# A transformer step: the down projection's seven products run from one ordered table, and one PSUM bank in it is added to x by VectorE

## The chip, the cores and the metric

The kernel runs on one core of one Trainium2 chip. Its metric is the device time of one execution in microseconds (us). Five engines matter: TensorE (PE, with its weight loads PEld), VectorE (DVE), ScalarE (ACT), GpSimd (POOL) and SyncE (SP, which here only issues DMAs). Each engine takes its instructions strictly in the order in which the program queues them; engines wait for each other by semaphores.

## The reference, cut to what matters

Two layers of a trunk on 256 context tokens and 1024 latent tokens. The change lies in the last matmul of each layer, the down projection of the feed-forward net:

```python
gate, up = jnp.split(h2 @ w_ffn_in[l], 2, axis=-1)
x = x + g2 * ((jax.nn.silu(gate) * up) @ w_ffn_out[l])     # (tokens, 2816) @ (2816, 1024)
```

## The kernel before

Everything is kept transposed: x is three tiles `xs[0]` (256 context tokens), `xs[1]` and `xs[2]` (512 latent tokens each), each with 8 blocks of 128 rows. The product `silu(gate) * up` was written to DRAM as FS, 22 slices of 128 rows. All matmuls are float32 in three passes: each operand is split into a rounded part hi (ACT, `copy` with a cast) and the rest lo (DVE, `tensor_sub`), and `product` runs lo*hi, hi*lo and hi*hi. A split is thus one ACT cast and then one DVE subtraction.

Per layer the down projection has three parts. `ffn_out(0)` and `ffn_out(2)` multiply slices 0 to 3 the plain way. The **middle part**, which the change rewrites, takes slices 4 to 19 in NC = 4 groups j of four slices. `ffn_out(NF - 2)` does the last two slices and the norm that follows. In the middle part the 1024 latent tokens are seen as two halves and a group's slices as two pairs, and for each pair of output blocks m and m + 4 (m = 0 to 3) seven products stand in for eight. I call one (j, m) a **step**; there are 16 in a layer. A step's TensorE order is the same in both kernels:

- `b21`, `t2`, `t1`: six 128x512 matmuls each; then the context product (24 matmuls of 128x256), then `t3`, `b22`, the next step's `b11`, and `t4`.
- `b11`, `t2`, `t3` and `t4` add up, one after the other, in one PSUM bank `a` (the chain). After each of them the bank's running sum has to be added to x before the next product of the chain may write it: after `b11` to block m of `xs[1]`, after `t2` (the second product) to block m of `xs[2]`, after `t3` (the third) to block m + 4 of `xs[2]`, after `t4` to block m + 4 of `xs[1]`.
- Bank `b` holds `b21`; bank `c` holds `t1`, is read, and then takes `b22` on top and is read again. The context bank is read in two halves.

`onto` (L1506) is such a read on DVE, x += bank * gate, in one instruction. `onto2` (L1510 to L1512) does it in two: ACT scales the bank into a tile `u` (L1511), POOL adds `u` to x (L1512). Before the change the chain's second and third reads use `onto2`.

Each step needs two weight slabs, split hi/lo into `w` tiles (a ring of 4): the plain slab `raw`, and one of four sums of its quarters, which POOL makes **in place** in the same `raw` tile (L190 to L192), so that the sums wait for the plain slab's DVE subtraction and the second split waits for the sums. `raw` has 2 buffers.

Each group needs eight operands of 128x1024 (`slots`, 12 in a ring): `b11`, `b21`, `b22` and the context's `c` are loaded from FS and halved in place by `halve` (ACT L1461, DVE L1462); `t1` to `t4` come from eight POOL subtractions (`op_sum`, L1479) into two `q` tiles and are split by `split` (ACT L109, DVE L110), each in two halves of 512. The POOL subtractions read the loaded `b11`, `b21`, `b22`, so `halve` of these has to wait for them. `out7` writes out by hand at which step the next group's loads, sums and splits stand. Inside the middle part every engine follows the order of the program text (`manual_schedule`); ahead of it and behind it only PE does, and a scheduler places the rest. DMAs of the middle part are issued by SP, in order.

Of the kernel before, what the change touches and what calls it, by code (L numbers as in the profile page):

```python
# [50 lines left out]
def build(tc, d):  # L51
# [60 lines left out]
    queue, ready, steps = [], [], []  # L112
# [62 lines left out]


    def out_sums(src):
        raws = []

        def load():  # L180
            raws.append(raw_slab(src))

        def plain():
            w = wtile()
            split(w[:, 0], w[:, 1], raws[0])
            ready.append(w)

        def quarters():
            r = raws[0].rearrange("p (q c) -> p q c", q=4)
            G.tensor_add(r[:, 3], r[:, 1], r[:, 3])  # L190
            G.tensor_sub(r[:, 0:2], r[:, 3:4].to_broadcast([P, 2, 256]), r[:, 0:2])
            G.tensor_sub(r[:, 1:3], r[:, 1:3], r[:, 0:1].to_broadcast([P, 2, 256]))  # L192

        def sums_():
            w = wtile()
            split(w[:, 0], w[:, 1], raws[0])
            ready.append(w)

        steps.append((load, plain, quarters, sums_))

    def want(l):
# [22 lines left out]
        for f in range(4):  # L224
            add(d["w_fo"][l, f * P:(f + 1) * P])
        for j in range(NC):
            for m in range(4):
                out_sums(d["w_fs"][l, j, m])
        for f in range(4, 6):
            add(d["w_fo"][l, f * P:(f + 1) * P])  # L230
# [343 lines left out]
    for l in range(DEPTH):  # L574
# [890 lines left out]
        def op_load(j):  # L1465
            f = 4 + 4 * j
            for kind, x, c in (("b11", 0, 1), ("b21", 2, 1), ("b22", 2, 2)):
                ld(operand(j, kind)[:, 1], rows_of(f + x, 2, c))
            qs[j] = [qpool.tile([P, 4, 512], F32, tag="q", bufs=2, name=nm("q")) for _ in range(2)]
            for i in range(2):  # L1470
                nc.sync.dma_start(qs[j][i][:, 0], FS[l][f + i, :, CH[2][0]:])


        def op_sum(j, n):
            i, n = divmod(n, 4)
            q = qs[j][i]
# [4 lines left out]
        def op_t(j, kind, part=(0, 1)):  # L1481
            t = ops.get((j, kind))
            if t is None:
                t = operand(j, kind)
            for i in part:
                split(t[:, 0, i], t[:, 1, i], qs[j][i][:, {"t1": 0, "t3": 1, "t2": 2, "t4": 3}[kind]])

        def op_c(j):
            ld(operand(j, "c")[:, 1], rows_of(4 + 4 * j, 4, 0))

        def op_h(j, kind):
            halve(ops[j, kind])
# [26 lines left out]
        def out1(j, m):  # L1519
            w = ready.pop(0)  # L1520
            pa_ = fpsum(512)
            product(pa_, wq(w, 0), opd(j, "b11"))
            onto(1, m, pa_)
            return w, pa_
# [3 lines left out]
        def out7(j, m, w, pa_):  # L1528
            s_ = ready.pop(0)
            last = (j, m) == (NC - 1, 3)  # L1530
            nj = j + 1 if j + 1 < NC else None
            cur = steps.pop(0) if steps and not last else None

            def do(at, *work):
                if nj and m == at:
                    for x in work:
                        x()

            def ctx():
                pc = psum()  # L1540
                for u in range(2):
                    a = wq(w, u) + wq(w, 2 + u)
                    mm3(pc[:, u * 256:(u + 1) * 256],
                        [a[i] + (ops[j, "c"][:, 0, i], ops[j, "c"][:, 1, i]) for i in range(4)])
                for u in range(2):
                    onto(0, m + 4 * u, pc[:, u * 256:(u + 1) * 256])

            pb, pc = fpsum(512), fpsum(512)
# [251 lines left out]
```

## Time and profile before

| | us |
|---|---|
| median of 3 runs (3018.08 to 3023.95) | 3021.41 |
| the profiled execution's own time | 3017.62 |
| its span, first to last instruction | 3015.5 |
| middle part of layer 0, by the PE timeline 1260.42 to 1479.87 | 219.45 |
| middle part of layer 1, 2743.20 to 2964.93 | 221.73 |

The span is cut by the clock of the trace: times below are us from its start. The middle part begins with its first matmul of `b11` and ends with the first matmul of the last `ffn_out`. "[1.42 <-DVE ft L1462]" behind a row means that the engine stood idle for 1.42 us before it and that DVE's instruction of line 1462, which writes `ft`, ended the wait. In the trace `ft` is an operand, `f` a bank, `ps` the context bank, `w` a split slab.

### The profile page before, as it was taken

Reading aid. Unit: us, or ns where it says so; the run is one execution under the profiler, and the core shown is the slowest. Engines: PE = TensorE matmul, PEld = TensorE weight load, DVE = VectorE, ACT = ScalarE, POOL = GpSimd, SP = SyncE. Lnnn points to the kernel's source line nnn. Section 1 sums busy time; section 2 is a strip of 40 time slices with the busy share of each in tenths; the row PEclk is TensorE's granted clock in tenths of the full one; section 3 lists DMA queues with packets and bytes.
Section 4 is the critical chain, followed back from the end, with each engine's and each line's share of the span. In section 5 each row is a group of like instructions: output and inputs, shape, how many; then the busy total and the mean of one; then the engine's idle time right before and its main releaser. Section 6 shows DMA issues by size and latency. Waiting matters only on the chain.

```text
span 3015.5 us, 41230 instructions
## 1 busy us (share of the span) xinstructions
PE 2871.2 (95%) x15608; PEld 2452.5 (81%) x15608; DVE 2007.7 (67%) x3157; ACT 1210.4 (40%) x2047; POOL 998.2 (33%) x980
## 2 busy tenths in 40 slices
PE   7999999999999999998999999999999999999997
PEld 4888898888888888877777888888888888887776
DVE  6777787685666554777868677776856533356777
ACT  4523687264223233233442237762622223332342
POOL 1222200035443332376512222001444433315663
PEclk9999999999999999999999999999999999999999
DMA  6576523543333233422235665444434312251212
GB/s 229 155 225 186 175 72 112 180 137 109 124 110 123 91 102 133 147 76 96 91 105 161 206 170 150 107 135 135 149 107 133 101 62 69 69 211 63 91 67 84
DMA packets 164406, 380.63 MB, mean 126 GB/s; under 512 B 20576, under 2 KB 56688, under 8 KB 163952
## 3 DMA queue, kind: packets, MB, share of 16 engines
q1 hardware_dynamic: 119680, 274.00, 29.1%
q0 software_dynamic: 44240, 103.84, 10.2%
q8 instruction: 122, 2.00, 0.3%
q14 instruction: 76, 0.62, 0.1%
q10 hardware_dynamic: 288, 0.16, 0.0%
HBM read 281.97 MB, written 95.95 MB: 125 GB/s over the span
## 4 chain that ended last, share of the span: by engine, by line
PE 66%; DVE 15%; issue 6%; POOL 5%; DMA 4%; ACT 4%; SPq 0%; DVEq 0%; POOLq 0%; ACTq 0%
PE f L1286 30%; PE f L249 15%; PE pa L249 6%; PE pa L489 4%; PE S L429 3%; PE ps L447 3%; DVE w L110 2%; PE ps L249 2%; POOL q L1479 2%; PE ps L967 1%; DVE stt L433 1%; DVE ft L110 1%; DMA x<-XS 1%; ACT E L436 1%; DVE ft L1462 1%
## 5 line engine op out<-in xcount | busy, mean ns | idle before, releaser
L110 DVE TENSOR_TENSOR w<-raw,w 128x1024 fp32r<-128x1024 f32 x278 | 356.2, 1283 | 284.6 <-ACT w L109 284.0
L1286 PE MATMUL f<-h,w 128*128 128x512 f32 x2112 | 506.3, 390 | 1.1 <-ACT pc L1234 1.1
L109 ACT CAST w<-raw 128x1024 fp32r<-128x1024 f32 x278 | 289.8, 1050 | 489.9 <-POOL raw L192 116.6
L1286 PEld LDWEIGHTS f<-h,w 128*128 128x128 f32 x2112 | 392.4, 188 | 82.1 <-ACT pc L1234 1.9
L1286 PE MATMUL f<-ft,w 128*128 128x512 f32 x1344 | 324.5, 396 | 30.3 <-DVE ft L1462 14.8
L1286 PEld LDWEIGHTS f<-ft,w 128*128 128x128 f32 x1344 | 249.6, 190 | 95.0 <-DVE ft L1462 19.9
L1286 PE MATMUL f<-T,w 128*128 128x512 f32 x1080 | 264.8, 394 | 15.0 <-DVE pc L1389 12.0
L1286 PEld LDWEIGHTS f<-T,w 128*128 128x128 f32 x1080 | 201.7, 188 | 65.1 <-DVE pc L1389 16.1
L1227 POOL DMA_DIRECT2D FS<-sg x132 | 72.8, 552 | 541.7 <-DVE sg L1358 222.2
L249 PE MATMUL pa<-h,w 128*128 128x512 f32 (+1 forms) x1296 | 248.4, 352 | 0.8 <-DVE vn L667 0.8
L249 PEld LDWEIGHTS pa<-h,w 128*128 128x128 f32 x1296 | 211.3, 191 | 32.4 <-DVE vn L667 1.0
L489 PE MATMUL pa<-w,h 128*128 128x512 f32 x912 | 218.6, 397 | 12.5 <-DVE w L110 12.0
L433 DVE TENSOR_REDUCE stt<-S 128x1 f32<-128x1280 f32 x128 | 189.9, 1487 | 57.3 <-PE S L429 57.3
L249 PE MATMUL f<-mix,w 128*128 128x512 f32 (+1 forms) x1152 | 225.0, 355 | 0.0
L489 PEld LDWEIGHTS pa<-w,h 128*128 128x128 f32 x912 | 171.9, 191 | 52.8 <-DVE w L110 10.0
L249 PEld LDWEIGHTS f<-mix,w 128*128 128x128 f32 x1152 | 189.8, 189 | 29.5
L436 ACT ACTIVATE E<-S,stt 128x1280 f32<-128x1280 f32 x128 | 170.5, 1332 | 40.9 <-DVE stt L433 40.9
L447 PE MATMUL ps<-vt,pt 128*128 128x128 f32 x1280 | 178.0, 279 | 5.3 <-ACT pt L973 5.2
L249 PE MATMUL f<-ft,w 128*128 128x512 f32 (+1 forms) x864 | 173.7, 362 | 5.7 <-DVE x L1107 5.7
L249 PEld LDWEIGHTS f<-h,w 128*128 128x128 f32 x1392 | 172.7, 192 | 3.3
L249 PE MATMUL f<-h,w 128*128 128x256 f32 x1392 | 174.1, 283 | 0.0
L429 PE MATMUL S<-kb,aq 128*128 128x512 f32 (+1 forms) x624 | 162.7, 377 | 9.7 <-ACT E L436 4.7
(247 smaller groups left out, 4877.4 us busy)
## 6 DMA issues: line engine op xcount, KB each, us to landing
raw<-w_fi SPq DMA_DIRECT2D x112, 512.0 KB, 3.8
ra<-w_adaT SPq DMA_DIRECT2D x96, 256.0 KB, 2.8
FS<-sg POOLq DMA_DIRECT2D x88, 256.0 KB, 2.3
kb<-KS SPq DMA_DIRECT2D x52, 320.0 KB, 6.6
raw<-w_adaT SPq DMA_DIRECT2D x32, 512.0 KB, 4.0
raw<-w_fs SPq DMA_DIRECT2D x32, 512.0 KB, 3.9
ft<-FS SPq DMA_DIRECT2D x32, 512.0 KB, 6.0
raw<-w_in SPq DMA_DIRECT2D x20, 512.0 KB, 3.6
```

Of the source, the lines that this page charges most:

```text
L109: S.copy(hi, src)
L110: V.tensor_sub(lo, src, hi.bitcast(F32))
L249: PE.matmul(ps, lhsT=a, rhs=b, start=(i == 0), stop=(i == n - 1))
L429: PE.matmul(ps[:, o:o + n], lhsT=aq[:, m, q0:q0 + P], rhs=kb[m][1 - p][:, o:o + n], start=(p == 0), stop=(p == 1))
L433: V.reduce_max(st[:, m:m + 1], ps[:, :nkey], axis=AX.X, negate=True)
L436: S.activation(E, ps[:, :nkey], AF.Exp, bias=st[:, m:m + 1], accum_out=st[:, 2 + m:3 + m])
L447: PE.matmul(o[:, :P], lhsT=pt[:, i * P:(i + 1) * P], rhs=vt(b + i), start=(b + i == 0), stop=(b + i == nk - 1))
L489: PE.matmul(ps, lhsT=a[:, y], rhs=wk[:, z], start=(k == 0 and x == 0), stop=(k == KD - 1 and x == 2))
L967: PE.transpose(T_["tp", b][:, x * P:(x + 1) * P], T_["E"][0][:, (4 * b + x) * P:(4 * b + x + 1) * P], ident)
L1227: nc.gpsimd.dma_start(FS[l][f, :, t0:t0 + n], sg)
L1286: PE.matmul(ps, lhsT=y, rhs=z, start=(first and i == 0), stop=(i == 3 * len(a) - 1), skip_group_check=not first)
L1479: G.tensor_sub(q[:, o], x, y)
```

## The change

`out7`, `out1`, `out_sums` and their helpers go. The order of the middle part now stands in one table, PLAN: four rows for m = 0 to 3, each a list of short names that `steps` walks through; each name is one instruction (or one product). A name's suffix says for which step (`+`, `++`, `+++`: 1 to 3 steps later, `-`: one earlier) or for which group (`.`, `:`, `;`: this one, the next, the one after) the instruction works. With the order these parts change:

- The chain's third read (U3) is one DVE instruction, `onto`, in place of ACT's scaling and POOL's addition. The second (U2 on ACT, A2 on POOL) stays as it was.
- POOL's sums of a slab's quarters go to a tile `s` of their own, in four instructions of 256 columns (before: one of 256, two of 512). The slab is loaded three steps ahead, its sums are made two steps ahead, the sums' split begins two steps ahead.
- The four `t` operands are split by one cast and one subtraction of 1024 columns each (before two of 512), out of one `q` tile for a group (before two, one for each slice).
- Of a group's operands, `b11` and `b21` are loaded two groups ahead, `b22`, `q` and `c` one; their casts and subtractions are spread over the steps one by one.
- The splits of the last `ffn_out`'s slabs and operands stand in the last group.

PE's products and their order stay as they were, but for the last step, whose context product moves to where it stands in all others. Line numbers after the change: DVE reads of banks L1511, slab splits L1497, operand splits L1462 (`t`) and L1469, POOL L1484 to L1490 (quarters), L1452 (operands), L1586 (A2).

```diff
-        def out7(j, m, w, pa_):
...
-            product(pb, wq(w, 2), opd(j, "b21"))
...
-            onto(1, m, pb)
-            do(0, lambda: op_load(nj))
-            product(pa_, wq(s_, 0), opd(j, "t2"), False)
-            if cur:
-                cur[2]()
-            onto2(2, m, pa_)
...
-            product(pa_, wq(s_, 1), opd(j, "t3"), False)
-            onto2(2, m + 4, pa_)
...
-            do(3, lambda: op_h(nj, "b21"), lambda: op_t(nj, "t1"))
...
+        def w_sum(g, n):
+            if not n:
+                sums_[g] = qpool.tile([P, 4, 256], F32, tag="s", name=nm("s"))
+            r, s_ = raws[g].rearrange("p (q c) -> p q c", q=4), sums_[g]
+            if n == 0:
+                G.tensor_add(s_[:, 3], r[:, 1], r[:, 3])
...
+        def w_split(key, src, part):
+            if part == "a":
+                slabs[key] = wtile()
+                S.copy(slabs[key][:, 0], src)
+            else:
+                V.tensor_sub(slabs[key][:, 1], src, slabs[key][:, 0].bitcast(F32))
...
+            elif name[0] == "P":
+                c, u, b = {"1": (1, 0, "a"), "2": (1, 0, "b"), "3": (2, 0, "c"), "4": (1, 4, "a"),
+                           "5": (2, 4, "c")}[name[1]]
+                onto(c, m + u, banks[b, g])
+            elif name in UDVE:
+                onto(2, m + 4, banks["a", g])
+            elif name[0] == "U":
+                banks[name, g] = qpool.tile([P, 512], F32, tag="u", bufs=2, name=nm("u"))
+                S.mul(banks[name, g], banks["a", g], mods[l][:, 5 * KD + m + (4 if name == "U3" else 0), 1:2])
...
+        def steps(j, loads=None):
+            for m, names in enumerate(PLAN):
+                for name in names.split():
...
+UDVE = ("U3",)
...
+    """b21 wa+ P4- q3: sd+ t2a: t2 P2 r0++ t1 U2 wd+ q7: cx P5 ld+++ A2 t2d: r1++ b21d: t3 r2++ r3++ b22 C0
+    U3 C1 b11+ sa++ P3 b22d: t4 cL:""",
```

The names of the table that the text uses: P1, P4 are the chain's first and last reads, P2 bank `b`'s, P5 and P3 bank `c`'s two, C0 and C1 the context bank's; `wa`/`wd` and `sa`/`sd` are cast and subtraction of the plain slab and of the sums; `b21d:` is the subtraction of the next group's operand `b21`; `r0` to `r3` are the quarters' sums, `q0` to `q7` the operands'; `ld` loads a slab, `cL:` an operand.

Two places in the order. First DVE, from the end of group 0's fourth step into group 1's first one. `x_10328`, `x_10332`, `x_10336` are xs[0], xs[1], xs[2]; a number behind `f_` is one bank; `ft_10367`, `ft_10368` and `ft_10370` hold operands, `q_...` the sums behind `t` operands. Before:

```order
L110 TENSOR_TENSOR w_11211<-raw_11054,w_11211 128x1024
L1462 TENSOR_TENSOR ft_10367<-ft_10367 128x1024
L110 TENSOR_TENSOR ft_10368<-q_10864,ft_10368 128x512
L110 TENSOR_TENSOR ft_10368<-q_10865,ft_10368 128x512
L1506 SCALAR_TENSOR_TENSOR x_10336<-f_11151,mod_83,x_10336 128x512
L1506 SCALAR_TENSOR_TENSOR x_10332<-f_11236,mod_83,x_10332 128x512
L1506 SCALAR_TENSOR_TENSOR x_10332<-f_11132,mod_83,x_10332 128x512
L1462 TENSOR_TENSOR ft_10368<-ft_10368 128x1024
L110 TENSOR_TENSOR w_11263<-raw_11158,w_11263 128x1024
L1506 SCALAR_TENSOR_TENSOR x_10332<-f_11253,mod_83,x_10332 128x512
L1506 SCALAR_TENSOR_TENSOR x_10336<-f_11254,mod_83,x_10336 128x512
```

Here `ft_10367` is `b21` of group 1, which PE multiplies first of all in the next step, and three subtractions of operands stand ahead of the first read (P1, `f_11236`) of the next step's chain. After:

```order
L1497 TENSOR_TENSOR w_11141<-s_11072,w_11141 128x1024
L1511 SCALAR_TENSOR_TENSOR x_10336<-f_11172,mod_83,x_10336 128x512
L1462 TENSOR_TENSOR ft_10368<-q_10877,ft_10368 128x1024
L1469 TENSOR_TENSOR ft_10368<-ft_10368 128x1024
L1511 SCALAR_TENSOR_TENSOR x_10336<-f_11134,mod_83,x_10336 128x512
L1511 SCALAR_TENSOR_TENSOR x_10328<-ps_11186,mod_83,x_10328 128x256 x2
L1511 SCALAR_TENSOR_TENSOR x_10336<-f_11172,mod_83,x_10336 128x512
L1511 SCALAR_TENSOR_TENSOR x_10332<-f_11235,mod_83,x_10332 128x512
L1462 TENSOR_TENSOR ft_10368<-q_10877,ft_10368 128x1024
L1511 SCALAR_TENSOR_TENSOR x_10332<-f_11134,mod_83,x_10332 128x512
L1462 TENSOR_TENSOR ft_10368<-q_10877,ft_10368 128x1024
L1511 SCALAR_TENSOR_TENSOR x_10332<-f_11256,mod_83,x_10332 128x512
```

Now `b21` is a step further up, P1 (`f_11235`) stands directly behind the step's other reads, and the operand split after it is `t3`'s; the read of `f_11134` in the fifth row is U3, which DVE did not have before.

Second, POOL over the third step of group 0 (`raw` and `s` are a slab's quarters, `q` operands, `x_10336` the additions to xs[2]). Before:

```order
L190 TENSOR_TENSOR raw_10957<-raw_10957 128x256
L191 TENSOR_TENSOR raw_10957<-raw_10957 128x512
L192 TENSOR_TENSOR raw_10957<-raw_10957 128x512
L1512 TENSOR_TENSOR x_10336<-x_10336,u_11069 128x512
L1479 TENSOR_TENSOR q_10865<-ft_10370,q_10865 128x512
L1512 TENSOR_TENSOR x_10336<-x_10336,u_11118 128x512
L1479 TENSOR_TENSOR q_10865<-q_10865,ft_10367 128x512
L1479 TENSOR_TENSOR q_10865<-ft_10370,q_10865 128x512
```

After:

```order
L1452 TENSOR_TENSOR q_10877<-ft_10367,q_10877 128x512
L1484 TENSOR_TENSOR s_11072<-raw_10986 128x256
L1452 TENSOR_TENSOR q_10877<-ft_10367,q_10877 128x512
L1586 TENSOR_TENSOR x_10336<-x_10336,u_11081 128x512
L1486 TENSOR_TENSOR s_11072<-s_11072,raw_10986 128x256
L1488 TENSOR_TENSOR s_11072<-raw_10986 128x256
L1490 TENSOR_TENSOR s_11072<-raw_10986,s_11072 128x256
```

The addition of the chain's third read is gone, the quarters belong to a later slab, and the operands' sums are done a step sooner.

## Rows read from the trace of the kernel before

**Rows 1.** Windows (us, busy us of each engine, clock, DMA): layer 0's middle part, four steps, layer 1's.

```profile
1260.42:1479.87 219.45, 205.19 (x1058) 171.81 (x1057) 156.09 (x184) 81.26 (x103) 139.28 (x101) 0.99 0.26 85
1376.31:1432.81 56.50, 51.29 (x266) 42.57 (x265) 41.34 (x50) 21.52 (x30) 39.74 (x28) 1.00 0.23 80
2743.20:2964.93 221.73, 205.71 (x1058) 171.81 (x1056) 157.26 (x186) 80.17 (x102) 138.53 (x101) 0.99 0.24 80
```

**Rows 2.** Timeline of PE in a step without a wait (start, us, instructions).

```profile
1337.55 9.71 PE L1286 MATMUL f<-ft,w 128*128 128x512 f32 x42
1347.10 3.04 PE L249 MATMUL ps<-ft,w 128*128 128x256 f32 x24
1349.97 1.32 PE L1286 MATMUL f<-ft,w 128*128 128x512 f32 x5
```

**Rows 3.** Waits of PE in layer 0's middle part (us, times, longest).

```profile
PE f L1286 <- DVE ft L1462: 7.7, 6, 1.5
PE f L1286 <- DVE x L1506: 5.1, 5, 1.1
```

**Rows 4.** Timeline of PE from group 1 to group 2.

```profile
1370.93 1.43 PE L1286 MATMUL f<-ft,w 128*128 128x512 f32 x5 [1.42 <-DVE ft L1462]
1373.45 3.02 PE L1286 MATMUL f<-ft,w 128*128 128x512 f32 x12 [1.10 <-DVE x L1506]
...
1380.83 0.96 PE L1286 MATMUL f<-ft,w 128*128 128x512 f32 x3 [0.55 <-DVE ft L110]
1383.06 8.38 PE L1286 MATMUL f<-ft,w 128*128 128x512 f32 x35 [1.27 <-DVE ft L1462]
```

**Rows 5.** Timeline of DVE in the same stretch.

```profile
1368.58 2.29 DVE L1462 TENSOR_TENSOR ft<-ft 128x1024 fp32r<-128x1024 f32 x1 [1.19 <-POOL q L1479]
1370.80 1.28 DVE L110 TENSOR_TENSOR ft<-q,ft 128x512 fp32r<-128x512 f32 x2
1372.00 2.06 DVE L1506 SCALAR_TENSOR_TENSOR x<-f,mod,x 128x512 f32<-128x512 f32 x3
...
1380.69 2.31 DVE L1462 TENSOR_TENSOR ft<-ft 128x1024 fp32r<-128x1024 f32 x1
```

**Rows 6.** Windows: three us after two waits at the end of group 0.

```profile
1317.00:1320.00 3.00, 3.00 (x8) 2.35 (x8) 3.00 (x4) 0.35 (x1) 0.37 (x1) 0.54 0.33 124
```

**Rows 7.** Timeline of DVE around 1395.

```profile
1395.25 1.22 DVE L110 TENSOR_TENSOR w<-raw,w 128x1024 fp32r<-128x1024 f32 x1
```

**Rows 8.** Timeline of POOL in the same stretch.

```profile
1395.34 2.28 POOL L1479 TENSOR_TENSOR q<-q,ft 128x512 f32<-128x512 f32 x1
1397.58 1.28 POOL L1512 TENSOR_TENSOR x<-x,u 128x512 f32<-128x512 f32 x1
```

**Rows 9.** Line 1506 over the whole trace: shortest/median/longest ns.

```profile
L1506 DVE SCALAR_TENSOR_TENSOR x<-f,mod,x x160: 734/746/754, 1262.6 to 2965.1; 128x512 f32<-128x512 f32 x160
```

**Rows 10.** Groups of DVE in the four steps (busy us, mean ns, idle before).

```profile
L1506 DVE SCALAR_TENSOR_TENSOR x<-f,mod,x 128x512 f32<-128x512 f32 x21 | 15.1, 744 | 4.6 <-PE f L1286 4.6
L110 DVE TENSOR_TENSOR w<-raw,w 128x1024 fp32r<-128x1024 f32 x9 | 12.1, 1347 | 1.5 <-ACT w L109 1.4
L110 DVE TENSOR_TENSOR ft<-q,ft 128x512 fp32r<-128x512 f32 x8 | 7.2, 926 | 1.1 <-ACT ft L109 1.1
L1462 DVE TENSOR_TENSOR ft<-ft 128x1024 fp32r<-128x1024 f32 x4 | 7.0, 1761 | 3.3 <-POOL q L1479 3.3
L1506 DVE SCALAR_TENSOR_TENSOR x<-ps,mod,x 128x256 f32<-128x256 f32 x8 | 3.5, 477 | 4.6 <-PE ps L249 4.6
```

**Rows 11.** Groups of POOL in the four steps.

```profile
L1512 POOL TENSOR_TENSOR x<-x,u 128x512 f32<-128x512 f32 x8 | 11.2, 1401 | 0.5 <-ACT u L1511 0.5
...
L190 POOL TENSOR_TENSOR raw<-raw 128x256 f32<-128x256 f32 x4 | 2.9, 736 | 11.0 <-DVE w L110 11.0
```

**Rows 12.** Waits of all engines in the four steps.

```profile
ACT w L109 <- POOL raw L192: 13.1, 4, 4.6
```

**Rows 13.** DMA issues of layer 0's middle part (median us to landing).

```profile
ft<-FS SPq DMA_DIRECT2D x10, 512.0 KB, 5.3
```

More of the change, by code (lines that the diff above doesn't have):

```diff
@@ L110, in split @@
         V.tensor_sub(lo, src, hi.bitcast(F32))
-    queue, ready, steps = [], [], []
+    queue, ready = [], []
     pools = {}
@@ L173, in sums @@
         queue.extend([gate, up, rest])
[L177 to L199, printed above, removed]
     def want(l):
@@ L1462, in halve, with op_load, q_load @@
             V.tensor_sub(t[:, 1], t[:, 1].bitcast(F32), t[:, 0].bitcast(F32))
[L1465 to L1471, printed above, removed]
+        HALVES = {"b11": (0, 2, 1), "b21": (2, 2, 1), "b22": (2, 2, 2), "c": (0, 4, 0)}
+        SUMS = {"t1": 0, "t3": 1, "t2": 2, "t4": 3}
+        def op_load(j, kind):
+            x, n, c = HALVES[kind]
+            ld(operand(j, kind)[:, 1], rows_of(4 + 4 * j + x, n, c))
+        def q_load(j, i):
+            if not i:
+                qs[j] = qpool.tile([P, 2, 4, 512], F32, tag="q", name=nm("q"))
+            nc.sync.dma_start(qs[j][:, i, 0], FS[l][4 + 4 * j + i, :, CH[2][0]:])
         def op_sum(j, n):
             i, n = divmod(n, 4)
-            q = qs[j][i]
+            q = qs[j][:, i]
             b11, b21, b22 = (ops[j, k][:, 1, i].bitcast(F32) for k in ("b11", "b21", "b22"))
@@ L1479, in op_sum, with op_t @@
             G.tensor_sub(q[:, o], x, y)
-        def op_t(j, kind, part=(0, 1)):
+        def op_t(j, kind, part):
             t = ops.get((j, kind))
@@ L1517, in opd @@
             return [(t[:, 0, i], t[:, 1, i]) for i in range(2)]
[L1519 to L1524, printed above, removed]
-        def out7(j, m, w, pa_):
[L1529 to L1540, printed above, removed]
+        banks = {}
@@ L1656, in build @@
         ffn_out(0, fds[0])
-        op_load(0)
-        op_c(0)
+        steps(-2, True)
+        steps(-1, True)
         ffn_out(2, fds[1])
-        for n in range(8):
-            op_sum(0, n)
-        for kind in ("b11", "b21", "t2", "t1", "c", "t3", "b22", "t4"):
-            (op_t if kind[0] == "t" else op_h)(0, kind)
-        for x in steps.pop(0):
-            x()
-        steps[0][0]()
-        nxt = out1(0, 0)
-        man = ExitStack()
-        man.enter_context(tc.manual_schedule())
-        for j in range(NC):
-            for m in range(4):
-                nxt = out7(j, m, *nxt)
-            if j == NC - 2:
-                for x in range(2):
-                    ld(tf[:, x, 1], FS[l][NF - 2 + x])
-        man.close()
+        steps(-2, False)
+        steps(-1, False)
+        with tc.manual_schedule():
+            for j in range(NC):
+                steps(j)
+            for m, names in enumerate(PLAN):
+                for name in names.split():
+                    if name[-1] == "-" and m < name.count("-"):
+                        step(name.rstrip("-"), 4 * NC + m - name.count("-"))
+        ready.extend(slabs["f", x] for x in range(2))
         fts = [tf[:, x] for x in range(2)]
-        for x in fts:
-            halve(x)
         dq.close()
```

166 lines of the change are left out of this document (117 added, 49 removed).

## The prediction

> **What bounds the kernel now.** I read three things in turn: how long the middle part takes against what its matmuls need, what PE waits for there, and what makes the awaited engine late.
>
> The windows of the two middle parts [rows 1] are 219.45 and 221.73 us long. A step without a wait [rows 2] starts its 42 long matmuls at 1337.55 and its 24 short ones at 1347.10: 9.55 us, 1.364 for a product of six. The 24 short ones take 2.87 more, until the next long one at 1349.97. A step thus needs 9.55 + 2.87 = 12.42 us and 16 steps 198.7. The rest is loss: 219.45 - 198.7 = 20.7 us in layer 0, 221.73 - 198.7 = 23.0 in layer 1, **43.7 us in all, 1.4% of the time**. No order of the other engines can give more in these parts, since PE's work stays.
>
> All that PE waits for there is DVE [rows 3]: 7.7 us on the halving of loaded operands, 5.1 us on the adds to x. These are the idle times alone; PE also loses some time in restarting after each, and after a close pair of waits it ran for 3 us at a granted clock of 0.54 [rows 6], that is mostly at 1.2 in place of 2.4 GHz. All this is inside the 43.7.
>
> Where the waits stand tells their cause. From group 1 to group 2 [rows 4] PE stops four times. At 1370.93 it needs `b21` of the next group, whose subtraction DVE begins only at 1368.58, having waited for POOL, and which takes 2.29 us [rows 5]. Behind it DVE still has two `t1` subtractions (1.28) and then three adds (2.06), of which the chain's first read P1 holds up `t2`: PE stops again at 1373.45. At 1380.83 and 1383.06 it stops for `t3` and `b22` of the group that already runs. So DVE is not short of time, it has its work in the wrong place: in four steps of 56.50 us it is busy for 41.34 [rows 1].
>
> Part of that busy time is waiting too. The halving subtraction of 1024 columns takes 1761 ns on average, 9 slab subtractions 1347 [rows 10], though one alone takes 1.22 us [rows 7]. The POOL instruction that is queued at 1395.34, beside that subtraction, takes 2.28 us where the next one takes 1.28 [rows 8]: the two don't run at once, and the later one stands still until the earlier is through. The adds from PSUM never do this: 160 of them lie between 734 and 754 ns [rows 9]. I call the resource that subtractions and POOL share the gate.
>
> **The change part by part.** Four steps are the unit, a group.
>
> *DVE.* U3 adds 4 instructions to 20 of 0.746 us and 8 of 0.477. With 8 slab and 8 operand subtractions of 1.22 (the four `t` now one of 1024 columns instead of a pair that took 1.28, [rows 5]): 24 x 0.746 + 8 x 0.477 + 16 x 1.22 = 41.2 us. Queued back to back an add takes 0.66 ((2.06 - 0.746)/2, [rows 5]), so 48 instructions overlap by some 0.08 each: 37.4 us net, against 49.7 that PE needs. DVE fits with 12 us to spare, less what it waits at the gate.
>
> *POOL and the gate.* POOL loses 4 adds of 1.28. The quarters become 16 of 0.736 [rows 11] in place of 4 of 0.736 and 8 of 1.28: 11.8 against 13.2 us. Eight operand sums of 1.28 stay. POOL: 11.8 + 5.1 + 10.2 = 27.1 us, before 13.2 + 10.2 + 10.2 = 33.6 (busy 39.74 with its waits, [rows 1]). With DVE's subtractions (19.5; before 8 + 4 of 1.22 and 4 pairs of 1.28, 19.8) the gate is needed for 46.6 us of a group against 53.4 of 56.50 before. It was 95% full and would be 94% full in 49.7 us: this is the tight resource of the new order.
>
> *ACT* gets rid of 4 scalings and is busy for 21.52 of 56.50 [rows 1]; its casts stop waiting for the sums in place (13.1 us a group, [rows 12]), since these are now a step ahead. I cost this at nothing either way: hidden behind PE.
>
> *Loads.* SP gets the same DMAs, other places. The nearest one to its use is the context operand: issued when the third step's last `b11` is through (9.70 + 1.36 = 11.06), landed 5.3 us after issue [rows 13], so at 4.0 of the fourth step; its cast stands behind `t1`'s there (done near 4.6). Hidden, and if it were late by more than about 3 us, DVE would hold U3 up. The two loads that are put two groups ahead reach SP's queue before x is loaded, while SP waits for room for x anyway: nothing.
>
> *Does the new order leave a wait?* Within a step the products begin at 0 (b21), 1.36 (t2), 2.73 (t1), 4.09 (context), 6.97 (t3), 8.33 (b22), 9.70 (next b11), 11.06 (t4). Reads can start some 0.2 us after their product. The operands of the next group are ready long ahead: `b11` after its second step, `b21`, `b22`, `t2` after the third, `t1` and `c` in the fourth, `t3` early in the next group for 6.97, `t4` by about 3.2 for 11.06. That clears the operand waits. What is left is the adds of the chain. In the third step DVE has ahead of U3: P4, P2, P5 (0.66 each), `sd`, `wd`, `t2d`, `b21d` (1.14 each) and C0 (0.40), 6.9 us. Starting at 0.2, with waits of 0.6 to 0.8 at the gate behind three of the four subtractions and one for P5's or a cast's readiness, U3 starts near 9.8 and ends near 10.5, before t4 at 11.06. Starting at 1.0 (the second step ran late at the gate) with three waits of nearly a full POOL instruction (1.0 to 1.2), it ends at 11.5: 0.5 us late. In the fourth step P1, P4, P2, P5, `wd`, `sd`, `t1d`, `cd` come to 7.2 us, the same margin; there P1 stands first for t2 at 1.36 and can be late by 0.3 to 0.8 when `b22d` ended the third step late. The first and second steps hold only 8.7 and 7.7 us of DVE's work (5 and 7 adds, 4 and 2 subtractions, the context's two halves) and let it catch up. So a group loses between 0 and 1.3 us. I take the upper end, since the gate is as full as it was: 1.3 x 3 groups with a successor x 2 layers = 7.8 us; the last group has no next operands, and I take nothing there. At the head, DVE's work ahead of the first step is the same (eight operands, two slabs), so nothing; PE's stops in `ffn_out(2)` stay.
>
> Sum: 43.7 - 7.8 = **35.9 us less**: 3017.6 - 35.9 = 2981.7 by the profiled execution's time. The median of the runs before is 3.8 above that execution, so I expect 2985.5 for a median of runs. Bounds: 43.7 less (2974 and 2977.7) if no wait is left; below.
>
> **The rivals.**
>
> *DVE becomes the bound.* U3 goes from an engine that is busy 21.52 of 56.50 us to one that is busy 41.34. If DVE has no idle time to give, each of the 32 moved adds costs its full 0.66: 21 us back, 14.8 us less than before, 3002.8 (3006.6 for the median). For it: the gate at 94%, DVE's subtractions wait there and its queue is in order. Against it: 12 us net of slack in 49.7. The Trainium skill, "Perfetto Trace Analysis", section "Optimizing Scalar/DVE Operations", says that when DVE is saturated, moving work off it to ScalarE may make sense; the change does the opposite, and by that advice this rival would be the outcome. The busy shares above don't show DVE saturated.
>
> *Slower.* U3 is a new DVE deadline inside every step: t4 may not start before it ends. If U3 came late by L in each of 32 steps, PE loses 32 L. The gain is eaten at L = 43.7/32 = 1.37 us, and at 1.6 the kernel is 7 us slower, 3024 (3028). That needs U3 to end at 12.4 or later of a step of 12.42, two full waits at the gate more than I count, every time; the longest single wait seen is about 1.1 us (2.31 against 1.22, [rows 5]). Unlikely.
>
> *The change doesn't do what it says.* POOL is what made `b21` late (1.19 idle before 1368.58, [rows 5]); if its operand sums still end late, because its queue now holds sums of slabs two steps ahead that wait for a free `s` or a load, the operand subtractions wait as before and only order changes: no difference, 3017 to 3021. Against it: POOL has 6.5 us a group less to do, and the last operand sum now stands early in the third step, a step before its use.
>
> **How the numbers follow.** Forecast 0.75; DVE-bound, with about 15 us less, 0.15; no difference 0.05; slower 0.05. A measurement here can tell about 0.2% (6 us) from no change. Faster: 0.75 + 0.15 = 0.90; within 0.2%: 0.05; slower 0.05. The likeliest case by itself, on the median's scale, lies between 2978 (nothing left of the 43.7) and 2997 (two and a half times the loss I take). The range adds the 3.8 us between execution and median below, and reaches to the DVE-bound case above: 2974 to 3006.
>
> **What would show it.** Right: both middle parts near 203 us long (198.7 + 3.9); PE's waits on operand halving gone, a few on adds to x (U3, P1) of under 1 us in the third and fourth steps; no half-clock stretch; POOL near 27 us busy a group plus its waits; subtractions on DVE still above 1.22 us on average. DVE-bound: PE waits for the adds in most steps, 0.5 to 0.7 each, and DVE near 100% busy there. Wrong altogether: waits of PE on operands, or DVE idle on POOL for over 1 us ahead of U3.

## The result, and the profile after

The changed kernel takes 2980.86 us (median, 2973.67 to 2984.5); in the same session the kernel before took 3022.52 us (3018.08 to 3023.95). The ratio is 0.9862, 95% interval 0.984 to 0.9883: 1.4% faster. The prediction was 2985.5 us in 2974 to 3006, with 0.90 for faster. The profiled execution took 2980.07 us, 37.5 less than that of before; 35.9 was forecast.

The windows of the changed kernel's middle parts, with four steps between them (columns as in [rows 1]):

```profile
1264.20:1464.20 200.00, 199.58 (x1058) 171.91 (x1056) 160.18 (x187) 70.69 (x75) 115.92 (x96) 1.00 0.27 86
1369.26:1418.90 49.64, 49.64 (x264) 42.73 (x263) 42.15 (x49) 16.94 (x18) 33.81 (x29) 1.00 0.19 62
2725.90:2925.84 199.94, 199.52 (x1057) 171.92 (x1056) 160.55 (x188) 69.55 (x74) 116.21 (x96) 1.00 0.25 81
```

The middle parts are 19.45 and 21.79 us shorter than in [rows 1], 41.2 together. The four steps take 49.64 us instead of 56.50, and PE is busy in all of it. The clock is 1.00, so the stretch of [rows 6] is gone. The span is only 37.2 shorter because the rest of the program differs from profile to profile: the first middle part begins at 1264.20 instead of 1260.42. In the changed kernel and e1, e2 and e4 to e7 below, whose programs up to there are all but the same, this beginning lies anywhere between 1258.2 and 1264.2. So the length of the middle parts is the sharper measure, and I compare by it.

The waits of PE in layer 0's middle part of the changed kernel; layer 1's gives the same single row:

```profile
PE f L1255 <- DVE x L1511: 0.4, 1, 0.4
```

[rows 3] has eleven waits there, and leaves out a third row of the same view, two waits on the splits of `t`:

```profile
PE f L1286 <- DVE ft L110: 1.1, 2, 0.5
```

The PE timeline where that wait stands, in the last step:

```profile
1447.61 6.29 PE L1255 MATMUL f<-ft,w 128*128 128x512 f32 x27
1454.32 3.06 PE L1255 MATMUL f<-ft,w 128*128 128x512 f32 x12 [0.42 <-DVE x L1511]
```

And DVE there (timeline): the halving of the last `ffn_out`'s operand (L1431) waits for ACT and then holds up the add behind it.

```profile
1452.11 1.49 DVE L1431 TENSOR_TENSOR ft<-ft 128x1280 fp32r<-128x1280 f32 x1 [1.43 <-ACT ft L1430]
1453.52 2.06 DVE L1511 SCALAR_TENSOR_TENSOR x<-f,mod,x 128x512 f32<-128x512 f32 x3
```

DVE's groups in the four steps, beside those of [rows 10] (busy us, mean ns, idle before):

```profile
L1511 DVE SCALAR_TENSOR_TENSOR x<-f,mod,x 128x512 f32<-128x512 f32 x24 | 17.8, 747 | 4.4 <-PE f L1255 4.1
L1469 DVE TENSOR_TENSOR ft<-ft 128x1024 fp32r<-128x1024 f32 x4 | 6.7, 1665 | 0.0
L1497 DVE TENSOR_TENSOR w<-raw,w 128x1024 fp32r<-128x1024 f32 x5 | 6.5, 1296 | 0.0
L1497 DVE TENSOR_TENSOR w<-s,w 128x1024 fp32r<-128x1024 f32 x4 | 6.1, 1522 | 0.4 <-ACT w L1495 0.4
L1511 DVE SCALAR_TENSOR_TENSOR x<-ps,mod,x 128x256 f32<-128x256 f32 x8 | 3.6, 476 | 2.7 <-PE ps L218 2.7
```

The halvings no longer wait for POOL (0.0, before 3.3). DVE waited for PE before as well (4.6 + 4.6 us in [rows 10], now 4.1 + 2.7); what is gone is its idle time behind ACT and POOL, 5.8 us there and 0.4 here. The subtractions are still longer than the 1.22 us of [rows 7].

### The profile page after: what moved, and what is told of

It is laid out like the page before. It is cut to its first block, busy times and chain, and to the rows that moved or that the text cites. A ratio compares the mean times of both kernels' runs of the same rounds, so it can differ in the third digit from the quotient of the medians.

```text
span 2978.3 us, 41223 instructions
## 1 busy us (share of the span) xinstructions
PE 2865.6 (96%) x15608; PEld 2457.3 (83%) x15608; DVE 2019.1 (68%) x3157; ACT 1187.8 (40%) x1983; POOL 957.2 (32%) x980
## 5 line engine op out<-in xcount | busy, mean ns | idle before, releaser
L110 DVE TENSOR_TENSOR w<-raw,w 128x1024 fp32r<-128x1024 f32 x210 | 265.4, 1266 | 270.1 <-ACT w L109 269.7
L109 ACT CAST w<-raw 128x1024 fp32r<-128x1024 f32 x210 | 218.4, 1050 | 360.1 <-POOL raw L159 107.7
L1255 PE MATMUL f<-ft,w 128*128 128x512 f32 x1344 | 312.7, 390 | 0.8 <-DVE x L1511 0.8
L1511 DVE SCALAR_TENSOR_TENSOR x<-f,mod,x 128x512 f32<-128x512 f32 x192 | 142.0, 747 | 46.4 <-PE f L1255 44.6
```

What stands on the lines that cost most here:

```text
L109: S.copy(hi, src)
L110: V.tensor_sub(lo, src, hi.bitcast(F32))
L1255: PE.matmul(ps, lhsT=y, rhs=z, start=(first and i == 0), stop=(i == 3 * len(a) - 1), skip_group_check=not first)
L1511: V.scalar_tensor_tensor(xs[c][:, m], in0=ps, scalar=mods[l][:, 5 * KD + m, COND[c]:COND[c] + 1], in1=xs[c][:, m], op0=ALU.mult, op1=ALU.add)
```

## The experiments

Each ratio is to the kernel before, timed in the same session. "Lost" is the length of both middle parts less twice 198.7, the need of PE that the prediction worked out (its 43.7 and the 43.8 here differ by rounding). "A part" is one layer's middle part.

| run | median us | ratio to before (interval) | middle parts us | lost us |
|---|---|---|---|---|
| before | 3022.52 | | 219.45, 221.73 | 43.8 |
| changed | 2980.86 | 0.9862 (0.984 to 0.9883) | 200.00, 199.94 | 2.5 |
| e1 | 2983.79 | 0.9867 (0.9853 to 0.9882) | 200.98, 200.99 | 4.6 |
| e2 | 2979.31 | 0.9858 (0.9842 to 0.9874) | 200.82, 200.73 | 4.2 |
| e3 | 3010.72 | 0.9958 (0.9943 to 0.9972) | 212.85, 215.41 | 30.9 |
| e4 | 2975.68 | 0.9839 (0.9825 to 0.9854) | 199.45, 199.48 | 1.5 |
| e5 | 2994.66 | 0.9911 (0.9894 to 0.9927) | 208.29, 208.28 | 19.2 |
| e6 | 2980.25 | 0.9862 (0.9847 to 0.9877) | 200.97, 200.94 | 4.5 |
| e7 | 2986.21 | 0.9877 (0.9862 to 0.9892) | 204.94, 204.98 | 12.5 |
| e8 | 3017.81 | 0.9984 (0.9975 to 0.9994) | 217.86, 219.50 | 40.0 |
| e9 | 2989.79 | 0.9894 (0.988 to 0.9907) | 203.91, 205.49 | 12.0 |
| e10 | 3009.17 | 0.9956 (0.9942 to 0.9969) | 212.71, 215.81 | 31.1 |
| e11 | 2967.05 | 0.9816 (0.9803 to 0.983) | 198.72, 198.72 | 0.0 |
| e12 | 2977.18 | 0.9851 (0.9833 to 0.9868) | 202.57, 202.58 | 7.8 |

**e1: the new table, U3 back on ACT and POOL.** A3 is POOL's add of U3; the same in all four rows.

```diff
-UDVE = ("U3",)
+UDVE = ()
-    ... r2++ U3 r3++ b11+ q0: P3 ...
+    ... r2++ U3 r3++ A3 b11+ q0: P3 ...
```

> The table's order is kept, but the chain's third read goes back to ACT's scaling and POOL's addition (right behind, on POOL). The changed kernel has 41.2 us less in its two middle parts than the one before (200.0 and 199.9 against 219.45 and 221.73). Theory 1 (the order did it: operand subtractions ahead of their products, sums ahead): PE still waits little, middle parts of 200 to 203 us each, 36 to 41 us less than before. Theory 2 (the gate did it: POOL's work that DVE took over is what made room): a group then needs the gate for 46.6 + 4 x 1.28 = 51.7 us, more than the 49.7 of PE, so at least 2.0 us for each of 6 groups come back and most likely more, middle parts of 206 us or longer, at most 29 us less than before.

Windows of layer 0's middle part:

```profile
1262.15:1463.13 200.98, 200.41 (x1057) 171.68 (x1056) 156.29 (x173) 81.38 (x91) 145.58 (x112) 1.00 0.27 86
```

Only 1.0 us a part comes back, with POOL busy for 145.58 us instead of 115.92. So 39.2 of the 41.2 us stay without U3 on DVE, and 2.0 belong to its engine, given this table. The 39.2 belong to the order together with the table's other parts (the slabs' sums earlier and in a tile of their own, `t` split in one piece); e6 and e9 below take some of these apart.

**e2: U2 on DVE as well.**

```diff
-UDVE = ("U3",)
+UDVE = ("U2", "U3")
-    ... U2 wd+ A2 cx P5 ...
+    ... U2 wd+ cx P5 ...
```

> The chain's second read is put on DVE as well; POOL then adds nothing to x. DVE's net work rises from 37.4 to 40.0 us of 49.7 in a group, the gate falls from 46.6 to 41.5. Theory 1 and theory 2: nothing is left to win but about 1.2 us in each middle part, so within 3 us of the changed kernel, 39 to 44 us less than before. Theory 3 (DVE is at its limit): PE waits for adds in the third and fourth steps, 0.5 us or more in each, 8 us or more given back.

Windows of layer 0's middle part:

```profile
1260.74:1461.56 200.82, 199.98 (x1057) 171.86 (x1056) 170.01 (x205) 60.06 (x59) 87.43 (x80) 1.00 0.28 86
```

DVE is now busy for 170.01 of 200.82 us and PE loses 0.8 more a part. DVE is not the bound, even with sixteen more adds a part.

**e3: the kernel before, U3 on DVE.**

```diff
-            onto2(2, m + 4, pa_)
+            onto(2, m + 4, pa_)
```

> The kernel before, its order kept, with the chain's third read as one DVE instruction. Theory 1: the operand subtractions stand where they stood, PE's waits on them stay, at most 10 us less than before, or a few us more since DVE has 2.6 us more to do in a group. Theory 2: the gate is needed for 53.4 - 5.1 = 48.3 us of 49.7, so it fits, and 20 us or more are saved.

The waits of PE in layer 0's middle part:

```profile
PE f L1286 <- DVE ft L1462: 3.8, 3, 1.3
PE f L1286 <- DVE x L1506: 3.2, 4, 1.0
PE f L1286 <- DVE ft L110: 1.6, 3, 0.5
```

It saves 6.6 + 6.3 = 12.9 us, between the two theories. POOL, freed of four adds a group, has b21's sums done sooner (at the turn to group 2 DVE waits 0.53 us for them where it waited 1.19, [rows 5]), and the three waits on `b21` among the six on L1462 in [rows 3] are gone; the three on `b22` are still there. What U3's engine is worth thus depends on the order: 12.9 us in the old one, 2.0 in the table. The two parts of the change don't add up.

**e4: b21's last halving from the third step to the fourth, behind P3.**

```diff
-    ... t2d: r1++ b21d: t3 r2++ ...
+    ... t2d: r1++ t3 r2++ ...
-    ... C1 P3 sa++ t4 P1+ t3d:
+    ... C1 P3 b21d: sa++ t4 P1+ t3d:
```

> The changed kernel with one name moved: the subtraction of the next group's b21 from the third step to the fourth, behind P3, so that it ends near or after the time when PE wants b21. Theory 1: PE waits there for the operand's subtraction once in each of 6 groups, 0.7 to 1.5 us with the restart, 4 to 9 us given back, 33 to 38 us less than before. Theory 2: the gate's load is the same, nothing changes, 40 to 43 us less than before.

Timeline of DVE at the end of a fourth step, and of PE there:

```profile
1357.81 1.22 DVE L1469 TENSOR_TENSOR ft<-ft 128x1024 fp32r<-128x1024 f32 x1
1358.94 0.75 DVE L1511 SCALAR_TENSOR_TENSOR x<-f,mod,x 128x512 f32<-128x512 f32 x1
```

```profile
1354.81 7.43 PE L1255 MATMUL f<-ft,w 128*128 128x512 f32 x32
```

The expected loss did not come: the halving is through at 1359.03 and PE runs on through the turn of the group. It takes its bare 1.22 us there, where in the third step of the changed kernel it took 2.32, and the parts are the shortest so far.

**e5: U3's add behind P3's.** In all four rows of the table.

```diff
-    ... r1++ C1 b22 r2++ U3 r3++ b11+ q0: P3 sa++ t4 ...
+    ... r1++ C1 b22 r2++ r3++ b11+ q0: P3 U3 sa++ t4 ...
```

> The changed kernel with one edit: in all four rows of the table the add of U3 stands behind that of P3 on DVE, instead of ahead of it (b11's sum and P3 in between). In the changed kernel U3's add ends 9.3 to 9.5 us into a step and the product t4, which overwrites its bank, begins at 11.06, so 1.5 us are spare; P3's bank is filled only shortly before. Theory 1 (what the change saves is the order of the work against TensorE's demand, and U3's bank has a deadline with 1.5 us to spare): U3 would end some 0.3 to 0.5 us after t4 wants to begin in each of the 32 steps; with the pipeline's refill 10 to 16 us come back, middle parts of 205 to 208 us, about 2991 to 2997 us. Theory 2 (TensorE's queue absorbs it, U3 has no deadline that matters here): middle parts of 200 to 201 us, the time of the changed kernel within 3 us.

Windows of layer 0's middle part, and one of PE's stops (timeline):

```profile
1258.17:1466.46 208.29, 203.73 (x1057) 170.83 (x1056) 160.55 (x189) 70.72 (x75) 111.26 (x96) 1.00 0.26 83
```

```profile
1348.45 1.88 PE L1255 MATMUL f<-ft,w 128*128 128x512 f32 x7 [0.21 <-DVE x L1511]
```

16.6 us come back, half a microsecond a step on average, a little over the upper end of what theory 1 said. By the starts of the matmuls, 15 steps of this part lose 0.41 to 0.49 us each. The last one, which has no next `b11` between `b22` and t4, loses 1.8. U3's deadline is real, and PE's queue does not absorb it: the slower rival had its mechanism right.

**e6: the slabs prepared one step ahead, as before.** Row 1 of four; the others alike.

```diff
-    """b21 P1 wa+ P4- r0++ t2 P2 r1++ wd+ t1 r2++ U2 r3++ ld+++ cx A2 P5 q1: t3 C0 q5: C1 b22 U3 q2: b11d:
-    b11+ sa++ t4 P3 q6: P1+""",
+    """b21 P1 wa+ P4- r0+ t2 P2 r1+ wd+ t1 r2+ U2 r3+ ld+++ cx A2 P5 sa+ q1: t3 C0 q5: C1 sd+ b22 U3 q2: b11d:
+    b11+ t4 P3 q6: P1+""",
```

> The changed kernel with the slabs' preparation pulled back to one step ahead: the four sums of a slab on POOL and the splits into its high and low parts on ACT and DVE stand all in the step just before the one that uses them, as in the kernel before, instead of being spread over two steps. Everything else, U3 on DVE and the place of the ffn operands, is as in the changed kernel. Theory 1 (the gain is the place of the ffn operands' halvings and sums, which no longer come behind TensorE's demand): the slabs were in time before too, so the middle parts stay at 200 to 204 us and the time within 5 us of the changed kernel. Rival (the deeper pipeline of the slabs is what clears the way): at least 15 us of the 41 come back, 215 to 220 us for both parts' loss together, 2996 us or more.

1.0 us a part comes back, so the deeper pipeline of the slabs is not where the gain lies. The sums keep their own tile here, so this run says nothing of ACT's wait for sums in place ([rows 12]); e9 does.

**e7: b21's last halving behind t3's, at the end of the fourth step.**

```diff
-    ... t2d: r1++ b21d: t3 r2++ ...
+    ... t2d: r1++ t3 r2++ ...
-    ... C1 P3 sa++ t4 P1+ t3d:
+    ... C1 P3 sa++ t4 P1+ t3d: b21d:
```

> The changed kernel with the last halving of b21 (on DVE) at the very end of the fourth step of a group, behind t3's. It ended 0.5 us before TensorE wanted it when it stood behind P3 in that step; at the end of the row it comes some 3 us after that. Theory 1 (a late operand stops TensorE for as long as it is late, and nothing takes that up again): each of the three groups with a successor in a middle part loses about 3 us, 18 to 20 us in both layers, middle parts of 208 to 210 us, about 2998 us: half of the change's gain gone by one misplaced instruction of 1.2 us. Rival (the later steps of the group have the time to catch up, as the prediction said of the first and second steps): the products behind run at once and the middle parts stay at 200 to 203 us.

The waits of PE in layer 0's middle part, and its window:

```profile
PE f L1255 <- DVE ft L1469: 4.6, 3, 1.5
PE f L1255 <- DVE x L1511: 0.4, 1, 0.4
```

```profile
1261.92:1466.86 204.94, 199.94 (x1057) 171.84 (x1056) 156.03 (x189) 70.42 (x75) 111.64 (x96) 1.00 0.27 84
```

One instruction of 1.2 us in the wrong place costs 10.0 us of the 41.2. Theory 1 is right that nothing takes the loss up again; its size was twice too large, since the halving was 1.5 us late and not 3.

**e8: the kernel before, operands sooner.** The sums, splits and halvings of the next group go to earlier steps, but in lumps, where the code had room for them.

```diff
-            do(1, lambda: op_sum(nj, 1))
-            do(2, lambda: op_sum(nj, 4), lambda: op_t(nj, "t2", (0,)))
-            do(3, lambda: op_sum(nj, 7))
-            if j and m == 0:
-                op_t(j, "t3")
-                op_h(j, "b22")
+            do(1, lambda: op_sum(nj, 1), lambda: op_sum(nj, 5))
+            do(2, lambda: op_sum(nj, 3), lambda: op_h(nj, "b11"))
+            do(3, lambda: op_h(nj, "b21"))
...
-            do(2, lambda: op_h(nj, "b11"))
+            do(2, lambda: op_t(nj, "t2"))
```

> The kernel before with its own structure (U3 still through ACT and POOL, slabs prepared one step ahead, plain function calls instead of a table); only the sums, splits and halvings of the next ffn operands are issued at sooner steps of a group: the sums of POOL from the first step on, b11, t2 and b22 in the third step, b21, t1, c and t3 in the fourth, t4 in the next group's first. Theory 1 (order): the waits of TensorE for operand halvings, which make most of the 43.7 us lost in the two middle parts, go, and 20 us or more are saved: middle parts of 208 to 212 us, 2995 to 3003 us. Rival (the work that the change takes from ACT and POOL, and U3's shorter chain, are what counts): at most as much as U3 on DVE alone gave, 13 us: middle parts of 213 to 219 us, 3008 to 3020 us.

The waits of PE in layer 0's middle part:

```profile
PE f L1286 <- DVE x L1506: 6.5, 5, 1.7
PE f L1286 <- DVE ft L110: 5.4, 3, 2.8
PE f L1286 <- ACT ft L109: 1.0, 1, 1.0
```

And one such wait, DVE's timeline and PE's:

```profile
1354.30 2.82 DVE L110 TENSOR_TENSOR ft<-q,ft 128x512 fp32r<-128x512 f32 x2
1357.05 0.74 DVE L1506 SCALAR_TENSOR_TENSOR x<-f,mod,x 128x512 f32<-128x512 f32 x1
```

```profile
1357.84 3.01 PE L1286 MATMUL f<-ft,w 128*128 128x512 f32 x12 [1.73 <-DVE x L1506]
```

Only 3.8 us are saved, and theory 1 as I had put it falls: "sooner" is not enough. The middle parts lie at the upper end of the rival's range (213 to 219); e9 tests its cause. The waits on b21 and b22 (L1462) are gone, and adds to x (6.5 us, before 5.1) and the splits of `t` (L110, 5.4 us, before 1.1) have taken their place: in the rows above, a pair of `t` subtractions stands on DVE ahead of an add that PE wants at once.

**e9: the same sums, the halvings one by one.** They are placed so that none stands directly ahead of an add that PE wants next: t2 behind the third step's last add, b22 early in the fourth step, t1 and c at its end, t3 and t4 early in the next group.

```diff
+            if j and m == 0:
+                op_t(j, "t3")
+            do(3, lambda: op_h(nj, "b22"))
...
+            if j and m == 0:
+                op_t(j, "t4")
...
+            do(2, lambda: op_t(nj, "t2"))
+            do(3, lambda: op_t(nj, "t1"), lambda: op_h(nj, "c"))
```

> The kernel before, with the operand sums as soon as in the run with the operands sooner, but with the halvings set one by one where no add that TensorE needs next stands behind them: b11 and b21 behind the step's first sum-of-slab work, t2 behind the step's last add in the third step, b22 at the start of the fourth, t1 and c at its end, t3 and t4 in the first half of the next group's first step. U3 still goes through ACT and POOL. In the run with the operands sooner the waits had moved from the halvings to the adds that stood behind pairs of halvings on DVE (11 waits on the adds, 14.7 us idle, 6 on halvings, 10.9). Theory 1 (the order decides: sooner, and nothing urgent behind): 25 us or more saved in the two middle parts, 204 to 209 us each, 2985 to 2997 us. Rival (in this structure POOL and the slabs' splits are late whatever the operands' places are, since U3's add sits on POOL): middle parts of 212 to 218 us, 3003 to 3018 us.

The waits of PE in layer 0's middle part:

```profile
PE f L1286 <- DVE x L1506: 3.1, 3, 2.0
```

And one of ACT there:

```profile
ACT w L109 <- POOL raw L192: 48.9, 15, 4.9
```

31.8 of the 43.8 us are saved in the old structure, with U3 on ACT and POOL, slabs one step ahead and sums in place: all waits on operands are gone, three on adds are left. The order alone does it, and this order means both: early enough, and not ahead of an urgent add. The wait of ACT for sums in place is as long as ever (48.9 us, 41.9 in the kernel before), so it was not what cost these 31.8 us.

**e10: e9 with U3 on DVE.** The one line of e3.

> As the run with the halvings one by one, and U3's bank is added to x by DVE. Theory 1 (order alone; U3's engine counts only where the order is bad): within 4 us of the run without it when that one is near 205 us a part. Rival (U3's engine is what clears POOL in this structure): 13 us or more below the run without it, as on the kernel before, middle parts 6 us shorter each.

Both theories missed: it is 19 us slower than e9. Timeline of DVE in a group's first step, and of PE there:

```profile
1378.37 2.82 DVE L110 TENSOR_TENSOR ft<-q,ft 128x512 fp32r<-128x512 f32 x2
1381.12 0.86 DVE L1506 SCALAR_TENSOR_TENSOR x<-ps,mod,x 128x256 f32<-128x256 f32 x2
1381.90 1.21 DVE L110 TENSOR_TENSOR w<-raw,w 128x1024 fp32r<-128x1024 f32 x1
1383.04 2.05 DVE L1506 SCALAR_TENSOR_TENSOR x<-f,mod,x 128x512 f32<-128x512 f32 x3
```

```profile
1377.25 4.27 PE L1286 MATMUL f<-ft,w 128*128 128x512 f32 x18
1383.92 2.88 PE L1286 MATMUL f<-ft,w 128*128 128x512 f32 x7 [2.41 <-DVE x L1506]
```

The 18 matmuls are t3, b22 and the next b11; t3's six are through near 1378.6. U3's add, the first of the three at 1383.04, could start then, but stands behind t4's two splits, the context's adds and a slab's subtraction; t4's product waits for it until 1383.92. In e9 the detour over ACT and POOL went round this queue. The chain's third read on DVE is good only where DVE's row has room in front of it, and the table has that: only one operand's subtraction, `t4`'s, stands ahead of U3 in a group's first step.

**e11: the table with the best places.** e4's move, and the last `ffn_out`'s operands halved behind P5 of the last group's third and fourth steps (ending the wait at 1454.32 above), and the first step's slabs summed and split ahead of `ffn_out(2)` instead of behind it.

```diff
+                                              j == -1 and 4 * j + m + len(sign) == 0 and sign[0] == "+" and
+                                              kind in ("wa", "wd", "sa", "sd", "r0", "r1", "r2", "r3")) != loads:
...
+                    if kind == "P5" and j == NC - 1 and m > 1:
+                        halve(tf[:, m - 2])
```

> The changed kernel with b21's last halving in the fourth step behind P3 (its middle parts were 199.5 us), and two edits around the middle part: the last ffn operands of a layer are halved behind P5 of the last group's third and fourth steps, and in the prologue the first slab's sums and splits go ahead of the splits of the other operands. Theory 1 (the middle part is at its floor of 198.7 plus under 1 us; what is left to save lies at its head and tail): middle parts of 199 to 200 us, the stop of TensorE ahead of the middle part (0.4 and 2.1 us idle, and a stretch at half the clock) shorter by 1 to 3 us a layer, 2970 to 2976 us. Rival (head and tail are set by the loads of x and the last operands, not by this order): 2975 to 2977 us, as without these two edits.

Windows of both middle parts, and of 30 us ahead of the first one, here and in the changed kernel:

```profile
1255.50:1454.22 198.72, 198.72 (x1057) 172.17 (x1056) 157.63 (x188) 70.54 (x75) 116.25 (x96) 1.00 0.27 87
2713.56:2912.28 198.72, 198.72 (x1058) 172.16 (x1056) 157.74 (x187) 69.59 (x74) 116.25 (x96) 1.00 0.25 81
...
1228.00:1258.00 30.00, 30.00 (x156) 25.65 (x156) 28.29 (x35) 8.33 (x10) 16.23 (x11) 1.00 0.12 35
```

```profile
1228.00:1258.00 30.00, 27.49 (x136) 23.12 (x135) 24.35 (x32) 8.42 (x9) 14.97 (x12) 0.94 0.14 52
```

PE never waits in a middle part: 198.72 us each is the floor of 198.7 that the prediction had from one clean step. The stop ahead of it (2.5 us idle) is gone too. The median of 2967.05 us lies below the 2970 to 2976 of theory 1. At 0.9816 this version beats both kernels: the interval ends at 0.983, where the changed kernel's begins at 0.984. Of the 13.8 us to the changed kernel the middle parts explain 2.5, and the stop in `ffn_out(2)` 2.5 idle in layer 0 and 1.8 in layer 1 and its restarts; the rest lies elsewhere in the program and is not settled. In the two profiled executions the first middle part begins at 1255.50 and at 1264.20, so 8.7 us of the difference lie ahead of it.

**e12: the same with U3 on ACT and POOL**, by e1's edit.

> The table with the best places, with U3's bank scaled by ACT and added by POOL (A3 in the table, four places behind U3). The measured effect of U3's engine so far: 12.9 us in the order of before, 1.0 us a part in the changed kernel's table, and 9 us a part the wrong way where halvings stood ahead of it on DVE. Theory 1 (with the order right, U3's engine no longer counts): middle parts of 198.7 to 200 us, within 2.5 us of the same table with U3 on DVE. Rival (at the floor, where PE never waits, the extra load on POOL and the gate shows): middle parts of 200.5 us or more, 4 us or more above.

Windows of layer 0's middle part, and PE's waits there:

```profile
1260.01:1462.58 202.57, 201.25 (x1058) 171.48 (x1056) 156.82 (x172) 80.96 (x91) 140.35 (x112) 1.00 0.26 85
```

```profile
PE f L1255 <- DVE x L1511: 0.7, 2, 0.3
PE f L1255 <- DVE ft L1469: 0.4, 2, 0.2
```

3.85 us a part are lost, 7.7 in both, as the rival said. b21's late halving had 0.5 us to spare in e4; with sixteen more POOL adds a part it is late in places, and adds are too. Idle are only 202.57 - 201.25 = 1.3 us; of the other 2.5 us, 2.2 go in the restarts of eight stops, four of them too short for the wait view (last section). So at the floor U3's engine is worth 7.7 us.

## Why the prediction was right, and where it was off

**Need and loss.** 12.42 us a step and 198.7 for sixteen: right, e11 measures 198.72. The 43.7 us of loss were all there was to win in the middle parts.

**Operand waits cleared by the order.** Right: the table without U3 on DVE gives 39.2 of the 41.2 us (e1), and the order alone, in the old code, 31.8 (e9). How the 7.4 us between divide over a better order, sums in a tile of their own and `t` split in one piece, no run shows. The prediction's phrase "it has its work in the wrong place" needs e8 beside it: sooner work in the wrong place on DVE only moves the wait to the adds.

**The loss left.** The term of 7.8 us (1.3 for each group with a successor) was the one mis-sized: 1.3 + 1.2 = 2.5 measured. Its places were wrong too. I put it on U3 in the third and P1 in the fourth step; what is left is P1 of the last step, 0.42 us idle in the last group where I took nothing (0.69 with its restart), and in each layer two delays of 0.2 us at P1 of second steps, which the wait view does not show. At the places where I took 7.8 us nothing was lost. The forecast of the sum (35.9) was thus 5.3 too small for the middle parts; the median came out 4.6 below the forecast.

**Why U3 was not late.** This is read from one step. Timeline of DVE in the third step of a group of the changed kernel; the step's context product begins at 1344.42 and the step itself 4.09 earlier, at 1340.33.

```profile
1340.54 0.75 DVE L1511 SCALAR_TENSOR_TENSOR x<-f,mod,x 128x512 f32<-128x512 f32 x1 [0.61 <-PE f L1255]
1341.21 1.22 DVE L1497 TENSOR_TENSOR w<-s,w 128x1024 fp32r<-128x1024 f32 x1
...
1343.00 1.32 DVE L1497 TENSOR_TENSOR w<-raw,w 128x1024 fp32r<-128x1024 f32 x1
...
1345.29 1.26 DVE L1462 TENSOR_TENSOR ft<-q,ft 128x1024 fp32r<-128x1024 f32 x1
1346.48 2.32 DVE L1469 TENSOR_TENSOR ft<-ft 128x1024 fp32r<-128x1024 f32 x1
1348.72 0.47 DVE L1511 SCALAR_TENSOR_TENSOR x<-ps,mod,x 128x256 f32<-128x256 f32 x1
1349.11 0.73 DVE L1511 SCALAR_TENSOR_TENSOR x<-f,mod,x 128x512 f32<-128x512 f32 x1
```

U3's add ends at 1349.84, 9.5 us into the step, where the prediction had 10.5 to 11.5. The four subtractions wait at the gate for 0, 0.10, 0.04 and 1.10 us beyond their 1.22, 1.2 in all; three waits of 0.6 to 1.2 were counted. DVE had begun the step waiting for PE (0.61), not behind it.

**The gate.** The count (46.6 of 49.7 us needed, 94%) was too dark. By the same count e1 needs 46.6 + 4 x 1.28 = 51.7 us a group, yet its groups take 200.98 / 4 = 50.2 and PE waits 0.4 us in a whole part. So durations of rows overstate how long the gate is held. One reason is in [rows 7, 8] and I had not drawn it: the POOL instruction queued at 1395.34 ends at 1397.62, and with 1.28 us of its own it would have run from 1396.34, while DVE's subtraction ends at 1396.47 by the profile; the two overlap by 0.13 us. With 16 subtractions a group there are at most 32 hand-overs, and such overlaps could hide some 4 us (an estimate from this one pair; no run here measures it apart). That the gate exists stands: subtractions average 1296 to 1665 ns in the four steps, and the 24 adds with one input in PSUM 747. The Trainium skill, "SBUF — State Buffer", section "Who interferes with whom", says that a DVE instruction with two SBUF inputs contends with a GpSimd one that reads SBUF, and that one with at most one SBUF input, outside the 2-port modes, does not. These numbers agree.

**ACT and POOL.** ACT was costed at nothing, and PE does not wait for it. But its casts still wait 6.8 us of the four steps for POOL's sums ([rows 12]: 13.1), where the prediction had these waits stop. POOL is busy for 33.81 us in the four steps, where 27.1 and its waits were expected.

**DVE as the bound.** Fell: 42.15 us busy in 49.64, its idle time is behind PE, and e2, with sixteen more adds a part on DVE, loses 0.8 us a part. The advice of the Trainium skill quoted with that rival ("Perfetto Trace Analysis", "Optimizing Scalar/DVE Operations") does not bite here: DVE at 160 of 200 us was not saturated, and in e12 the move off DVE lost 7.7 us.

**Slower.** Did not happen, but its mechanism exists: e5 shows U3's deadline inside each step, and e10 a U3 on DVE that is 2.4 us late in the first step of three groups. Its price was put too low: a stop costs more than its idle time (below).

**The change doesn't do what it says.** Fell: no halving waits for POOL in the four steps above.

**At head and between** the prediction took nothing, and said that the stops of `ffn_out(2)` stay: they stay, and e11 shows that a slab's early place removes them.

## What to carry to other kernels

When the awaited engine has idle time, look at what stands ahead of the awaited instruction in its queue, and give each step its deferrable work one instruction at a time behind the urgent one; moving it sooner in lumps just moves the wait (e8 against e9). Moving an instruction to another engine has no worth of its own: the same edit gave 12.9 us in one order, 2.0 in another, 7.7 in a third (e11 against e12), and took 19 in a fourth (e10). And count a deadline by rows of the step it lies in, with the slack to the next product, rather than by the share of a busy resource.

## What the runs showed of the hardware

A stop of PE costs about 0.3 us more than the idle time that the wait view shows. In e7's layer 0 part there are four stops with 204.94 - 199.94 = 5.0 us idle, and the part is 204.94 - 198.72 = 6.2 us over the floor: 1.2 us for four restarts. The starts of the matmuls show where this lies. In an undisturbed stretch they lie 0.227 us apart (1.364 / 6), while the row of each is 0.39 long. A matmul that starts up to 0.16 us late thus shows no idle time before it. And the second matmul behind each of these four stops starts another 0.11 us late. In e5 a stop with 0.21 us idle costs 0.48 in this way, and in e12 four of eight stops, with 0.07 or 0.08 us idle, cost some 0.34 each and are in no row of the wait view.

Stops of nearly one length left the clock alone or halved it. In e10 PE stops for 2.39 us before 1330.87 and for 2.41 before 1383.92; windows of three us a little after each show a granted clock of 1.00 after the first and of 0.50 (1.2 GHz of 2.4) after the second:

```profile
1384.60:1387.60 3.00, 3.00 (x9) 2.33 (x8) 1.67 (x3) 0.00 (x0) 0.89 (x1) 0.50 0.39 153
1331.20:1334.20 3.00, 3.00 (x15) 2.47 (x14) 2.51 (x4) 0.00 (x0) 1.24 (x1) 1.00 0.52 167
```

Three us at half the clock do 1.5 us of work, so the same lateness costs some 1.5 us more in one group than in another. Which of the two happens, these runs don't explain.
